# Last MLP of a two-layer trunk: blocks of the down projection in pairs, by seven products each

## The chip, the cores and the metric

One core of a Trainium2 chip runs the whole program. The metric is the time of one execution on the device in microseconds (us), the median of several runs.

## The reference, cut to what matters

Two layers; each has a token mixer and an MLP with squared ReLU. All data are float32; x is 512 tokens by 1024, the MLP's hidden width is 4096. The change is in the second layer's MLP, the last stage before the output:

```python
shift, scale, gate = ada_mod(c, ada_w[layer, 1], ada_b[layer, 1])    # three rows of 1024; gate has 1 added
u = x * (1.0 + scale) + shift
y = jnp.square(jax.nn.relu(u @ mlp_w1[layer] + mlp_b1[layer])) @ mlp_w2[layer] + mlp_b2[layer]
x = layer_norm(ALPHA * x + gate * y, ln_g[layer, 1], ln_b[layer, 1])
```

## The kernel before

Every large product is made of three: an operand x is split into a high part (a cast to float32r, on ACT) and a low part (x less its high part, on DVE), and PE adds up high x high, high x low and low x high in PSUM (`mm3`). A matmul multiplies a 128x128 block with 128x512.

`mlp` goes through the hidden width in eight blocks of 512. `up(b)` makes four chunks of 128 hidden units for all 512 tokens, 24 matmuls each; ACT makes relu (`r`) and its square, rounded, as high part (`hh`); DVE squares `r` again (`h`) and takes the low part (`hl`). `down(b)` multiplies them with 512 rows of w2: for each of four groups of 128 tokens and both halves of the 1024 columns twelve matmuls, 96 for the block, and DVE adds each result to `Y`. `up(b)` stands ahead of `down(b - 1)`.

Weights come in a list that `plan_weights` writes, a megabyte an entry. `w_dma` loads one into one of two buffers (`ws`), `w_pre` splits it (tiles `wh` and `wl`, four of 128x1024 each, or 128x512 tiles of the common pool `s2` for the entries in `wsmall`), `w_take` hands it to PE. The DMAs are all issued on SP's queue, in order; a load waits there for its buffer.

Beside the blocks run two things: `self.later` holds the residual (X times ALPHA times the norm's row, plus a row; 16 POOL steps on 128x512), taken up by `self.step`, two a chunk, so in block 1. `self.ada` holds the gate's sums over c (`ada_steps`, loads `ast`, sums `acc`, one half on DVE, one on ACT and POOL), taken up by `self.tick` from block 1 on; PE adds up over partitions at the end (`pada`). In the last block w2 is multiplied by the gate on POOL, and `Y` too, so that `down(7)` can add straight to X.

The pools give out buffers as they become free. The order within each engine is set by the scheduler of the tile layer, from the order in which the code issues and its own estimate of times; so instructions stand otherwise than in the code. All lines of the profile are L50, the helper's.

Of the kernel before, what the change touches and what calls it, by code (L numbers as in the profile page):

```python
# [8 lines left out]
F32 = mybir.dt.float32  # L9
F32R = mybir.dt.float32r  # L10
# [3 lines left out]
ALU = mybir.AluOpType  # L14
# [4 lines left out]
P = 128  # L19
D = 1024  # L20
S = 512
NT = S // P
# [12 lines left out]
WS_BUFS = 2  # L35
S2_BUFS = 42
PRED = mybir.dt.uint32


class InOrder:  # L40
# [33 lines left out]
class Trunk:  # L74
# [19 lines left out]
    def s2(self, name, dtype=F32):  # L94
        return self.sp.tile([P, S], dtype, tag="s2", name=name)
# [220 lines left out]
    def plan_weights(self):  # L316
        i = self.i
        L = []
        win = i["ev_w_in"][0]
        L += [("ch", win, 1024, 256), ("ch", win, 1280, 256), ("tok", win, 1536), ("tok", win, 1792),  # L320
              ("ch", win, 2048, 256), ("ch", win, 2304, 256), ("ch", win, 640, 128), ("ch", win, 768, 256)]

        def out(w, n):
            for h in range(2):
                for b in range(2):
                    L.append(("half", w, h, b, n))

        def mlp(l):
            w1, w2 = i["mlp_w1"][l], i["mlp_w2"][l]
            up = lambda b: [("ch", w1, b * 512, 256), ("ch", w1, b * 512 + 256, 256)]  # L330
            dn = lambda b: [("rows", w2, b * 512, 2 * l + 1), ("rows", w2, b * 512 + 256, 2 * l + 1)]
            L.extend(up(0))
            for b in range(1, 8):
                L.extend(up(b) + dn(b - 1))
            L.extend(dn(7))

        self.wsmall = set()

        def alternate(n0):
            for q in range(n0, len(L)):  # L340
                if (q - n0) // 2 % 2:
                    self.wsmall.add(q)

        n0 = len(L)
        out(i["ev_w_out"][0], 0)
        mlp(0)
        alternate(n0)
# [7 lines left out]
        out(i["od_w_out"][0], 2)  # L355
        mlp(1)
        alternate(n0)
        self.wlist, self.n_dma, self.n_split, self.n_take = L, 0, 0, 0
        self.wstage, self.wready = {}, {}

    def w_dma(self):
        d = self.wlist[self.n_dma]
        kind, w = d[0], d[1]
        if kind == "ch":
# [34 lines left out]
    def w_pre(self, eng=None):  # L399

        nc = self.nc
        if self.n_split >= len(self.wlist):
            return
        while self.n_dma < min(self.n_split + WS_BUFS, len(self.wlist)):
            self.w_dma()
        d = self.wlist[self.n_split]
        st = self.wstage.pop(self.n_split)
        kind = d[0]
        small = self.n_split in self.wsmall
# [18 lines left out]
        self.n_split += 1  # L428

    def w_take(self):  # L430
# [325 lines left out]
    def even(self):  # L756
# [341 lines left out]
    def mlp(self, l, X, rest, last):  # L1098
        nc, i = self.nc, self.i
        n = 2 * l + 1  # L1100
        nb = 8

        def up(b):
            hh, hl = self.u8("hh"), self.u8("hl")
            ws = self.w_take() + self.w_take()
# [10 lines left out]
            for f in range(4):  # L1116
                if b == 0:
                    part(f, 2, 4)
                else:
                    self.proj_ch(pts[f], ws[f])  # L1120
                if f % 2 == 0:
                    self.w_pre()
                col = 64 + l * 32 + b * 4 + f
                r, h2 = self.s2("r"), self.s2("h2")
                nc.scalar.activation(r, pts[f], AF.Relu, bias=self.colA[:, col:col + 1])
                nc.scalar.activation(hh[:, f], r, AF.Square)
                nc.vector.tensor_tensor(h2, r, r, op=ALU.mult)
                nc.vector.tensor_tensor(hl[:, f], h2, hh[:, f].bitcast(F32), op=ALU.subtract)
                if b:
                    self.step(2)  # L1130
                    if f % 2:
                        self.tick()
            return hh, hl

        def down(b, hh, hl, mid=None, after=None, byhalf=False):
            ws = self.w_take() + self.w_take()
            for t in range(NT):
# [26 lines left out]
                if not byhalf:  # L1164
                    for h in range(2):
                        nc.vector.tensor_tensor(Y[t][h], Y[t][h] if b else b2[h], pts[h], op=ALU.add)
                        if b == nb - 2:
                            nc.gpsimd.tensor_tensor(Y[t][h], Y[t][h], self.gates[n][h], op=ALU.mult)
                            nc.gpsimd.tensor_tensor(X[t][h], X[t][h], Y[t][h], op=ALU.add)
                else:  # L1170
# [5 lines left out]
                    self.tick()  # L1176

        b2 = self.bc(i["mlp_b2"][l:l + 1, :], f"b2{l}")
        Y = [[self.s2(f"Y{t}_{h}") for h in range(2)] for t in range(NT)]
        prev = up(0)  # L1180
        for b in range(1, nb):
            if b == 1 and last:
                self.ada = [self.ada_steps([(3, 4)], "g", True), self.ada_steps([(3, 5)], "v", True)]
            cur = up(b)
            down(b - 1, *prev)
            prev = cur
        self.tick(99)
        if last:
            g = self.bc(i["ln_g"][1, 1:2, :], "fg")
# [407 lines left out]
```

## Time and profile before

| | us |
|---|---|
| three runs | 1262.27, 1263.17, 1264.21 |
| profiled execution | 1266.51 |
| its span, first to last instruction | 1264.8 |
| PE / DVE / ACT / POOL busy in it | 1224.6 / 908.8 / 590.2 / 512.9 |
| granted TensorE clock, mean | 0.994 of 2.4 GHz |

The last MLP begins at about 901 us. A matmul's listed time overlaps the next one's: the distance of two starts says what one costs. The same holds for DVE and ACT, with a smaller overlap.

### The profile page before, as it was taken

The numbers are of one execution on the slowest core, as the hardware profiler recorded it, in microseconds if no ns is written. First come the engines' busy times: TensorE is split into PE (matmuls) and PEld (weight loads), VectorE is DVE, ScalarE is ACT, GpSimd is POOL, SyncE is SP. The second block draws the span as 40 slices with busy tenths as digits, with TensorE's granted clock in tenths as the row PEclk, the third lists the DMA queues.
The fourth block names the chain that finished last, engine by engine and source line by source line (L and its number), as shares of the span: only waits on it lengthen the run. The fifth ranks groups of instructions, "written<-read, shape, count | busy, mean of one in ns | idle before, by whom it ended". The sixth has DMA issues, their size and how long they took to land. (4 is left out here: it accounts for less than half of the span.)

```text
span 1264.8 us, 17847 instructions
## 1 busy us (share of the span) xinstructions
PE 1224.6 (97%) x6543; PEld 1044.2 (83%) x6543; DVE 908.8 (72%) x1423; ACT 590.2 (47%) x1044; POOL 512.9 (41%) x524
## 2 busy tenths in 40 slices
PE   6999899999999999999999999999899999999997
PEld 5787678888888888888999999887888788888886
DVE  7689898768877866879578878778768744543656
ACT  3476653452453544432567767753453342322321
POOL 3665523346330321474266558558437000000166
PEclk9999999999999999999999999999999999999999
DMA  9657416163666466524232332343262624232311
GB/s 316 186 199 267 173 61 198 56 230 119 240 224 233 145 195 227 182 67 124 81 101 85 92 93 52 113 153 106 79 233 72 211 67 133 81 117 70 133 34 67
DMA packets 126409, 177.52 MB, mean 140 GB/s; under 512 B 9270, under 2 KB 82644, under 8 KB 126322
## 3 DMA queue, kind: packets, MB, share of 16 engines
q1 hardware_dynamic: 126210, 176.33, 42.4%
q8 instruction: 52, 0.85, 0.3%
q14 instruction: 35, 0.29, 0.1%
q10 hardware_dynamic: 112, 0.05, 0.0%
HBM read 172.10 MB, written 4.26 MB: 139 GB/s over the span
## 5 line engine op out<-in xcount | busy, mean ns | idle before, releaser
L50 DVE TENSOR_TENSOR wl<-ws,wh 128x512 fp32r<-128x512 f32 (+1 forms) x255 | 269.3, 1081 | 67.7 <-ACT wh L50 63.4
L50 ACT CAST wh<-ws 128x1024 fp32r<-128x1024 f32 (+2 forms) x271 | 207.5, 808 | 200.5 <-PE p L50 81.4
L50 PE MATMUL p<-uh,wh 128*128 128x512 f32 (+1 forms) x576 | 206.2, 366 | 0.0
L50 PE MATMUL p<-uh,wl 128*128 128x512 f32 (+1 forms) x576 | 205.9, 365 | 0.0
L50 PE MATMUL p<-wh,hh 128*128 128x512 f32 (+1 forms) x516 | 201.0, 390 | 0.0
L50 PE MATMUL p<-wh,hl 128*128 128x512 f32 (+1 forms) x516 | 200.0, 388 | 0.0
L50 PE MATMUL p<-wl,hh 128*128 128x512 f32 (+1 forms) x516 | 199.9, 387 | 0.0
L50 PE MATMUL p<-ul,wh 128*128 128x512 f32 (+1 forms) x576 | 192.9, 366 | 0.0
L50 POOL TENSOR_TENSOR acc<-acc,ast 128x512 f32<-128x512 f32 x70 | 102.9, 1470 | 203.3 <-ACT ast L50 108.4
L50 DVE TENSOR_TENSOR h<-r 128x512 f32<-128x512 f32 x64 | 53.6, 840 | 123.6 <-ACT r L50 123.6
L50 PEld LDWEIGHTS p<-uh,wl 128*128 128x128 f32 x576 | 108.6, 189 | 17.5
L50 PEld LDWEIGHTS p<-uh,wh 128*128 128x128 f32 x576 | 108.6, 189 | 17.6
L50 PEld LDWEIGHTS p<-ul,wh 128*128 128x128 f32 x576 | 100.9, 189 | 17.4
L50 PEld LDWEIGHTS p<-wh,hh 128*128 128x128 f32 x516 | 96.9, 188 | 20.3 <-issue 0.2
L50 PEld LDWEIGHTS p<-wl,hh 128*128 128x128 f32 x516 | 96.9, 188 | 20.2 <-issue 0.5
L50 PEld LDWEIGHTS p<-wh,hl 128*128 128x128 f32 x516 | 96.9, 188 | 19.8
L50 ACT ACTIVATE r<-p,colA 128x512 f32<-128x512 f32 x64 | 43.8, 684 | 148.7 <-PE p L50 148.7
L50 POOL TENSOR_TENSOR ws<-ws,gate 128x512 f32<-128x512 f32 x16 | 25.0, 1597 | 210.6 <-DMA ws<-in_mlp_w_dram 210.6
L50 DVE TENSOR_TENSOR Y<-Y,p 128x512 f32<-128x512 f32 x96 | 64.8, 681 | 41.0 <-PE p L50 40.3
L50 ACT ACTIVATE ast<-ast,cs 128x512 f32<-128x512 f32 x70 | 49.9, 721 | 91.3 <-DMA ast<-in_ada_w_dram 91.3
L50 DVE SCALAR_TENSOR_TENSOR acc<-ast,cs,acc 128x512 f32<-128x512 f32 x70 | 82.5, 1179 | 13.2 <-DMA ast<-in_ada_w_dram 12.7
L50 POOL TENSOR_TENSOR ul<-u,uh 128x512 fp32r<-128x512 f32 x32 | 45.0, 1418 | 74.0 <-ACT uh L50 65.4
(320 smaller groups left out, 2681.2 us busy)
## 6 DMA issues: line engine op xcount, KB each, us to landing
ws<-in_mlp_w_dram SPq DMA_DIRECT2D x64, 1024.0 KB
ast<-in_ada_w_dram SPq DMA_DIRECT2D x160, 256.0 KB
ws<-in_od_w_in_dram SPq DMA_DIRECT2D x16, 1024.0 KB
ast<-in_ada_w_dram SPq DMA_DIRECT2D x16, 512.0 KB
ws<-in_ev_w_in_dram SPq DMA_DIRECT2D x7, 1024.0 KB
ws<-in_ev_w_out_dram SPq DMA_DIRECT2D x4, 1024.0 KB
nf<-fd SPq DMA_DIRECT2D x16, 256.0 KB
ws<-in_od_w_out_dram SPq DMA_DIRECT2D x4, 1024.0 KB
```

The costliest lines, as they stand in the source:

```text
L50: x = f(*a, **k)
```

## The change

In the last MLP blocks 0 to 5 are taken in three pairs. A pair's down projection is 512 tokens x 1024 hidden x 1024 columns; cut in half each way it is eight products of 256 x 512 x 512, and `winograd` makes it with seven, in Winograd's form of Strassen's method. Each product has a factor of the hidden values (`A11, S3, S1, S2, A12, A22, S4`) and one of the weights (`B11, T3, T1, T2, B21, T4, B22`); S and T are sums and differences of the quarters. `up(b, raw)` leaves the squares unsplit in float32 (`hr`), since sums are formed first; `factor` forms and splits them (`ha`, or `hah` and `hal`). `wino_b` forms and splits the weights' factors, with a second copy of one quarter (`wE`), loaded once more. Four pairs of PSUM banks hold the products; three are added to a second time. DVE adds the results to `acc` (U2, Q7, Q5, C11, D21, D12), and eight additions after the third pair make `Y` of them. Blocks 6 and 7 stay as they were, but now `up(6)` and `up(7)` stand together.

The residual steps move to blocks 2 and 3 (counted from 0), one a chunk; the gate's sums are taken up in blocks 4 to 6. Up weights of all blocks but 1 and 7 are split in tiles of 128x1024. The first MLP stays.

```diff
+WINOGRAD = (1,)
+WINO_B = ("B11", "T3", "T1", "T2", "B21", "T4", "B22")
+WINO_A = ("A11", "S3", "S1", "S2", "A12", "A22", "S4")
+WINO_SRC = {"B11": (0, 0), "T3": (0, 1), "B21": (1, 0), "B22": (1, 1)}
...
+            if l in WINOGRAD:
+                for g in range(0, 6, 2):
+                    L.extend(up(g) + up(g + 1) + [("wino", w2, g * 512, x) for x in WINO_B])
+                L.extend(up(6) + up(7) + dn(6) + dn(7))
+                for b in (n0 + 2, len(L) - 6, len(L) - 2):
+                    self.wsmall |= {b, b + 1}
+                return
...
+    def wino_b(self, which, st):
...
+        if which == "B11":
+            self.wB11 = st
+        elif which == "T3":
+            self.wE, self.wB12 = self.wE_next, st
+            for k in range(4):
+                sub(self.wE[k], self.wE[k], st[:, k])
+        if which == "T1":
+            for a in (0, 2):
+                x = self.wB12[:, a:a + 2, :]
+                sub(x, x, self.wB11[:, a:a + 2, :])
+                r += halves(self.wB12, a)
+            for k in range(4):
+                nc.vector.tensor_tensor(self.wE[k], self.wE[k], self.wB11[:, k], op=ALU.add)
+            return r
+        for a in (0, 2):
+            r += halves(self.wE if which in ("T3", "T2", "T4") else st, a)
+        if which == "B21":
+            for k in range(4):
+                sub(self.wE[k], st[:, k], self.wE[k])
+        return r
...
+            for q, (bank, on, to, bias) in enumerate(plan):
+                if len(ops) < min(q + 3, 7):
+                    ops.append(factor(WINO_A[len(ops)], H, len(ops)))
+                w = self.w_take()
+                self.w_pre()
+                if not on:
+                    pts[bank] = [self.ps("p2") for _ in range(2)]
+                for k in range(4):
+                    for t in range(2):
+                        tok = slice(t * P, t * P + P)
+                        lh, ll = [x[:, tok] for x in ops[q][k]]
+                        for n3, (x, y) in enumerate(((lh, w[k][0]), (lh, w[k][1]), (ll, w[k][0]))):
+                            nc.tensor.matmul(pts[bank][t], x, y, start=(not on and k == 0 and n3 == 0),
+                                             stop=(k == 3 and n3 == 2), skip_group_check=True)
...
+            for g in range(0, 6, 2):
+                H = [up(g, True)[0], None]
+                first = [factor(WINO_A[q], H, q) for q in range(2)]
+                H[1] = up(g + 1, True)[0]
+                if g == 2:
+                    self.ada = [self.ada_steps([(3, 4)], "g", True), self.ada_steps([(3, 5)], "v", True)]
+                winograd(g, acc, H, first)
```

What stands in the engines' order at the places that matter, before and after (names are tiles, numbers tell them apart; `p2` is a PSUM bank of the down projection):

PE before, the start of a token group of `down` in block 1: `wh`, `wl` weights, `hh`, `hl` hidden values.

```order
L50 MATMUL p2_10406<-wh_10200,hh_9795 128x512
L50 MATMUL p2_10406<-wl_10201,hh_9795 128x512
L50 MATMUL p2_10406<-wh_10200,hl_9796 128x512
L50 MATMUL p2_10407<-wh_10200,hh_9795 128x512
L50 MATMUL p2_10407<-wl_10201,hh_9795 128x512
L50 MATMUL p2_10407<-wh_10200,hl_9796 128x512
```

PE now, the start of the second pair's third product (T1 in `wh_10568`, S1 in `hah` and `hal`; p2_10719 and p2_10720 are the fourth product's):

```order
L55 MATMUL p2_10669<-wh_10568,hah_10557 128x512
L55 MATMUL p2_10669<-wl_10569,hah_10557 128x512
L55 MATMUL p2_10670<-wh_10568,hah_10557 128x512
L55 MATMUL p2_10670<-wl_10569,hah_10557 128x512
L55 MATMUL p2_10719<-wh_10614,ha_10609 128x512
L55 MATMUL p2_10720<-wh_10614,ha_10609 128x512
L55 MATMUL p2_10669<-wh_10568,hal_10558 128x512
L55 MATMUL p2_10670<-wh_10568,hal_10558 128x512
```

Matmuls with S1's low part have moved behind those with its high part and behind two of the next product.

DVE before, the gate's sum `acc` and the gate itself in `up(2)` (`h`, `hl` hidden values):

```order
L50 TENSOR_TENSOR h_10209<-r 128x512
L50 SCALAR_TENSOR_TENSOR acc_5_9989<-ast_5_3_0_10162,cs,acc_5_9989 128x512
L50 TENSOR_TENSOR hl<-h_10209,hh 128x512
L50 SCALAR_TENSOR_TENSOR acc_5_9989<-ast_5_3_1_10164,cs,acc_5_9989 128x512
L50 TENSOR_TENSOR h_10239<-r 128x512
L50 TENSOR_TENSOR hl<-h_10239,hh 128x512
```

DVE now, the same last two steps of `acc`, at the start of the third pair's products (`hr<-hr` form S2 and S1, `wl<-ws` is T1, `U` an accumulator, `ha` S2's low part, `hal` S1's):

```order
L55 TENSOR_TENSOR hr<-hr 128x4x256
L55 SCALAR_TENSOR_TENSOR acc_5_11012<-ast_5_3_0_11191,cs,acc_5_11012 128x512
L55 TENSOR_TENSOR hr<-hr 128x4x256
L55 TENSOR_TENSOR wl<-ws,wh 128x1024
L55 TENSOR_TENSOR U_9978<-U_9978,p_11221 128x512
L55 SCALAR_TENSOR_TENSOR acc_5_11012<-ast_5_3_1_11193,cs,acc_5_11012 128x512
L55 TENSOR_TENSOR U_9980<-U_9980,p_11222 128x512
L55 TENSOR_TENSOR wl<-ws,wh 128x1024
L55 TENSOR_TENSOR ha<-hr,ha 128x1024
L55 TENSOR_TENSOR hal<-hr,hah 128x512 x2
```

They have moved from an up phase to the place between S1's steps and the split of its low part.

ACT before, one block's last chunks and the casts behind them:

```order
L50 ACTIVATE r<-p_10778,colA 128x512
L50 ACTIVATE hh<-r 128x512
L50 ACTIVATE r<-p_10779,colA 128x512
L50 ACTIVATE hh<-r 128x512
L50 CAST wh<-ws 128x512 x8
```

ACT now, the last two chunks ahead of the third pair's products (`wE_11031`, `wE_11032` are T3's second half, `ast` the gate's loads):

```order
L55 ACTIVATE r<-p_11025,colA 128x512
L55 ACTIVATE hr<-r 128x512
L55 CAST wh<-wE_11031 128x512
L55 CAST wh<-wE_11032 128x512
L55 ACTIVATE r<-p_11026,colA 128x512
L55 ACTIVATE hr<-r 128x512
L55 ACTIVATE ast_4_3_0_11183<-ast_4_3_0_11183,cs 128x512
L55 ACTIVATE ast_4_3_1_11185<-ast_4_3_1_11185,cs 128x512
L55 CAST wh<-ws 128x1024 x2
```

Casts of weights have moved ahead of the last chunk's relu, and two of the gate's products stand behind its square.

## Rows read from the trace of the kernel before

**Rows 1.** Page: busy us (share) and count; tenths in 40 slices.

```profile
PE 1224.6 (97%) x6543; PEld 1044.2 (83%) x6543; DVE 908.8 (72%) x1423; ACT 590.2 (47%) x1044; POOL 512.9 (41%) x524
...
PE   6999899999999999999999999999899999999997
...
DVE  7689898768877866879578878778768744543656
```

**Rows 2.** Chain that ended last: start us, us, engine, tile, count.

```profile
995.14 255.74 PE p L50 x1128
...
1250.97 0.70 DVE X L50
```

**Rows 3.** Timeline of PE and ACT: start us, us, engine, instruction, idle before.

```profile
1060.31 0.39 PE L50 MATMUL p<-uh,wh 128*128 128x512 f32 x1
...
1065.74 0.39 PE L50 MATMUL p<-uh,wh 128*128 128x512 f32 x1
...
1059.14 1.06 ACT L50 CAST wh<-ws 128x1024 fp32r<-128x1024 f32 x1 [0.30 <-PE p L50]
...
1065.94 0.69 ACT L50 ACTIVATE r<-p,colA 128x512 f32<-128x512 f32 x1 [4.38 <-PE p L50]
1066.67 0.64 ACT L50 ACTIVATE hh<-r 128x512 fp32r<-128x512 f32 x1
...
1083.53 4.25 ACT L50 CAST wh<-ws 128x512 fp32r<-128x512 f32 x8
```

**Rows 4.** Timeline of DVE in the same block.

```profile
1060.61 1.22 DVE L50 TENSOR_TENSOR wl<-ws,wh 128x1024 fp32r<-128x1024 f32 x1
1061.75 0.68 DVE L50 TENSOR_TENSOR Y<-Y,p 128x512 f32<-128x512 f32 x1
...
1066.67 0.69 DVE L50 TENSOR_TENSOR h<-r 128x512 f32<-128x512 f32 x1 [3.10 <-ACT r L50]
1067.46 0.69 DVE L50 TENSOR_TENSOR hl<-h,hh 128x512 fp32r<-128x512 f32 x1
...
1084.39 2.49 DVE L50 TENSOR_TENSOR wl<-ws,wh 128x512 fp32r<-128x512 f32 x4
```

**Rows 5.** Timeline of PE at the gate's sums.

```profile
992.20 1.12 PE L50 MATMUL pada<-acc,ones 128*128 128x512 f32 x2 [0.58 <-POOL acc L50]
...
994.01 1.12 PE L50 MATMUL pada<-acc,ones 128*128 128x512 f32 x2 [0.69 <-DVE acc L50]
```

**Rows 6.** Timeline of POOL and DVE, with POOL busy and, last row, idle.

```profile
952.37 13.37 POOL L50 TENSOR_TENSOR X<-X,rB 128x512 f32<-128x512 f32 x8
...
989.16 2.99 POOL L50 TENSOR_TENSOR acc<-acc,ast 128x512 f32<-128x512 f32 x2 [13.57 <-ACT ast L50]
...
959.41 1.77 DVE L50 TENSOR_TENSOR wl<-ws,wh 128x512 fp32r<-128x512 f32 x1
961.11 1.78 DVE L50 SCALAR_TENSOR_TENSOR acc<-ast,cs,acc 128x512 f32<-128x512 f32 x1
...
976.65 0.74 DVE L50 SCALAR_TENSOR_TENSOR acc<-ast,cs,acc 128x512 f32<-128x512 f32 x1
```

**Rows 7.** Timeline of SP's issues and ACT: a weight load and its first cast.

```profile
978.02 3.84 SPq L50 DMA_DIRECT2D ws<-in_mlp_w_dram  x2
...
982.95 2.00 ACT L50 CAST wh<-ws 128x1024 fp32r<-128x1024 f32 x2 [6.44 <-DMA ws<-in_mlp_w_dram]
```

**Rows 8.** Timeline of PE after its longest wait near the last MLP.

```profile
889.71 1.30 PE L50 MATMUL pt<-ident,X 128*128 128x128 f32 x8 [3.26 <-DVE X L50]
...
891.23 0.63 PE L50 MATMUL pw<-wl,mh 128*128 128x512 f32 x1
891.66 0.63 PE L50 MATMUL pw<-wh,ml 128*128 128x512 f32 x1
...
894.08 0.40 PE L50 MATMUL pw<-wh,ml 128*128 128x512 f32 x1
```

More of the change, by code (lines that the diff above doesn't have):

```diff
@@ L321, in plan_weights, with alternate @@
               ("ch", win, 2048, 256), ("ch", win, 2304, 256), ("ch", win, 640, 128), ("ch", win, 768, 256)]
+        self.wsmall = set()
+        def alternate(n0):
+            for q in range(n0, len(L)):
+                if (q - n0) // 2 % 2:
+                    self.wsmall.add(q)
         def out(w, n):
@@ L335, in mlp @@
             L.extend(dn(7))
[L337 to L342, printed above, removed]
+            alternate(n0)
         n0 = len(L)
         out(i["ev_w_out"][0], 0)
+        alternate(n0)
         mlp(0)
-        alternate(n0)
         win = i["od_w_in"][0]
@@ L355, in plan_weights @@
         out(i["od_w_out"][0], 2)
+        alternate(n0)
         mlp(1)
-        alternate(n0)
         self.wlist, self.n_dma, self.n_split, self.n_take = L, 0, 0, 0
@@ L363, in w_dma @@
         kind, w = d[0], d[1]
+        if kind == "wino":
+            return self.wino_dma(*d[1:])
         if kind == "ch":
@@ L408, in w_pre @@
         kind = d[0]
+        if kind == "wino":
+            self.wready[self.n_split] = self.wino_b(d[3], st)
+            self.n_split += 1
+            return
         small = self.n_split in self.wsmall
@@ L428, in w_pre, with wino_dma, halves @@
         self.n_split += 1
+    def wino_dma(self, w, r0, which):
+        nc = self.nc
+        block = lambda r, c: w[r:r + 512, c:c + 512].rearrange("(k p) f -> p k f", p=P)
+        st = None
+        if which in WINO_SRC:
+            r, c = WINO_SRC[which]
+            st = self.wp.tile([P, 4, 512], F32, tag="ws", bufs=WS_BUFS, name="ws")
+            nc.sync.dma_start(st, block(r0 + 512 * r, 512 * c))
+        if which == "T3":
+            E = [self.s2(f"wE{k}") for k in range(4)]
+            for k in range(4):
+                nc.sync.dma_start(E[k], w[r0 + 512 + k * P:r0 + 512 + k * P + P, 512:1024])
+            self.wE_next = E
+        self.wstage[self.n_dma] = st
+        self.n_dma += 1
+    def wino_b(self, which, st):
+        nc = self.nc
+        sub = lambda o, a, b: nc.vector.tensor_tensor(o, a, b, op=ALU.subtract)
+        r = []
+        def halves(src, a):
+            hi, lo = [self.wp.tile([P, 2, 512], F32R, tag=x, name=x) for x in ("wh", "wl")]
+            if isinstance(src, list):
+                for j in range(2):
+                    nc.scalar.copy(hi[:, j], src[a + j])
+                    sub(lo[:, j], src[a + j], hi[:, j].bitcast(F32))
+            else:
+                nc.scalar.copy(hi, src[:, a:a + 2, :])
+                sub(lo, src[:, a:a + 2, :], hi.bitcast(F32))
+            return [(hi[:, j], lo[:, j]) for j in range(2)]
+        if which == "B11":
[18 more added lines that the diff above has]
+        return r
     def w_take(self):
@@ L1116, in up @@
             for f in range(4):
+                if f == 2 and len(ws) < 4:
+                    ws = ws + self.w_take()
+                if f % 2 == 0 and b and raw:
+                    self.w_pre()
                 if b == 0:
@@ L1128, in up @@
-                nc.vector.tensor_tensor(hl[:, f], h2, hh[:, f].bitcast(F32), op=ALU.subtract)
-                if b:
+                if not raw:
+                    h2 = self.s2("h2")
+                    nc.vector.tensor_tensor(h2, r, r, op=ALU.mult)
+                    nc.vector.tensor_tensor(hl[:, f], h2, hh[:, f].bitcast(F32), op=ALU.subtract)
+                if raw:
+                    self.step(b > 1)
+                elif b:
                     self.step(2)
-                    if f % 2:
-                        self.tick()
+                if f % 2 and b and (l not in WINOGRAD or b > 3):
+                    self.tick()
@@ L1133, in up, with factor @@
             return hh, hl
+        def factor(name, H, q):
+            a = [H[0][:, :, 0:256], H[0][:, :, 256:512]] + ([H[1][:, :, 0:256], H[1][:, :, 256:512]] if H[1] else [])
+            sub = lambda o, x, y: nc.vector.tensor_tensor(o, x, y, op=ALU.subtract)
+            if q % 3 < 2:
+                t = self.u8("ha", F32R, (2, 4, 256))
+                parts = [(slice(0, 4), t[:, 0], t[:, 1])]
+            else:
+                parts = [(slice(f, f + 2), *[self.s2(x, F32R).rearrange("p (k t) -> p k t", k=2) for x in ("hah", "hal")])
+                         for f in (0, 2)]
+            if name == "S3":
+                sub(a[1], a[0], a[1])
+            elif name == "S1":
+                sub(a[1], a[3], a[1])
+                nc.vector.tensor_tensor(a[0], a[0], a[1], op=ALU.add)
+            elif name == "S4":
+                sub(a[2], a[2], a[1])
+            src = a[{"A11": 0, "S3": 1, "S1": 0, "S2": 1, "A12": 2, "A22": 3, "S4": 2}[name]]
+            terms = []
+            for fs, hi, lo in parts:
+                nc.scalar.copy(hi, src[:, fs])
+                sub(lo, src[:, fs], hi.bitcast(F32))
+                terms += [(hi[:, k], lo[:, k]) for k in range(fs.stop - fs.start)]
+            return terms
@@ new lines, in winograd @@
+        def winograd(g, acc, H, first):
+            ops = list(first)
+            pts = {}
+            plan = [("1", False, "U2", None), ("7", False, "Q7", None), ("5", False, "Q5", 1), ("6", False, "U2", None),
+                    ("1", True, "C11", 0), ("7", True, "D21", 0), ("5", True, "D12", 1)]
+            for q, (bank, on, to, bias) in enumerate(plan):
+                if len(ops) < min(q + 3, 7):
+                    ops.append(factor(WINO_A[len(ops)], H, len(ops)))
+                w = self.w_take()
+                self.w_pre()
+                if not on:
+                    pts[bank] = [self.ps("p2") for _ in range(2)]
+                for k in range(4):
+                    for t in range(2):
[4 more added lines that the diff above has]
+                                             stop=(k == 3 and n3 == 2), skip_group_check=True)
+                ops[q] = None
+                for t in range(2):
+                    if (to, t) in acc:
+                        nc.vector.tensor_tensor(acc[to, t], acc[to, t], pts[bank][t], op=ALU.add)
+                        continue
+                    acc[to, t] = self.s2(f"{to}{t}")
+                    if bias is None:
+                        nc.vector.tensor_copy(acc[to, t], pts[bank][t])
+                    else:
+                        nc.vector.tensor_tensor(acc[to, t], b2[bias], pts[bank][t], op=ALU.add)
@@ L1178, in mlp @@
         b2 = self.bc(i["mlp_b2"][l:l + 1, :], f"b2{l}")
[L1179 to L1185, printed above, removed]
-            prev = cur
+        if l in WINOGRAD:
+            acc = {}
+            for g in range(0, 6, 2):
[5 more added lines that the diff above has]
+                winograd(g, acc, H, first)
+            for t in range(2):
+                for x, y in (("D12", "U2"), ("D21", "U2"), ("Q7", "Q5"), ("Q7", "U2")):
+                    nc.vector.tensor_tensor(acc[x, t], acc[x, t], acc[y, t], op=ALU.add)
+            Y = [[acc["C11", t], acc["D12", t]] for t in range(2)] + [[acc["D21", t], acc["Q7", t]] for t in range(2)]
+            del acc
+            prev = up(6)
+            cur = up(7)
+            down(6, *prev)
+            prev = cur
+        else:
+            Y = [[self.s2(f"Y{t}_{h}") for h in range(2)] for t in range(NT)]
+            prev = up(0)
+            for b in range(1, nb):
+                cur = up(b)
+                down(b - 1, *prev)
+                prev = cur
         self.tick(99)
```

15 lines of the change are left out of this document (9 added, 6 removed).

## Prediction

> **What bounds the kernel now.** I read the page's share of busy time first: PE is busy 97% of the span and DVE 72%, and in the 40 slices PE stays at 9 through the last seven while DVE falls to 3 to 6 [rows 1]. A busy PE can hide waits, so I went to the chain that ended last. Its largest piece lies in the last MLP: 1128 matmuls in 255.74 us with nothing between them, then a few DVE steps to the end [rows 2]. That is 255.74 / 1128 = 0.2267 us a matmul of 512 columns; PE waits for nobody there, so each such matmul taken out should give back 0.2267 us, as long as PE goes on waiting for nobody. What could make it wait is DVE and ACT, which split weights and hidden values into high and low parts. Their costs I read from the timelines of one quiet block.
>
> ACT takes 0.53 us for a cast of 512 columns (eight in 4.25) and 1.06 for 1024; relu and square take 0.73 and 0.63, and relu starts 0.20 after the last matmul of its chunk (24 matmuls from 1060.31 to 1065.74, relu at 1065.94) [rows 3]. DVE lists 1.22 us for 1024 columns and 0.69 for 512, but its next instruction starts after 1.14 (1060.61 to 1061.75) and 0.60 (four in 2.49, less the overlap of the last); only a step that reads the one right in front of it starts after 0.79 (1066.67 to 1067.46) [rows 4].
>
> **What is removed.** A pair of blocks had 192 matmuls of down projection; seven products of 24 make 168. Three pairs: 72 matmuls, 72 x 0.2267 = **16.3 us** off PE, all of them on the chain [rows 2].
>
> Before, the gate's two column sums made PE wait 0.58 us for POOL and 0.69 for DVE at 992 and 994 [rows 5]. In the change the last of these sums stand on DVE and POOL in the third pair's first two products, and PE's two sums behind the last chunk of block 6, some 50 us later. The waits go: **1.3 us**. PE's own work for them stays.
>
> **What is added, and what covers it.** Per pair, DVE now has, by the order's rows, 27 instructions of 1024 columns and 42 of 512: 27 x 1.14 + 42 x 0.60 = 56.0 us; before it was 8 and 48, 37.9 us. PE needs 360 x 0.2267 = 81.6 us for the pair, so on average DVE still fits. But the work is uneven: in the seven products (7 x 5.44 = 38.1 us) DVE has 14 of 1024 and 32 of 512, 35.2 us. Cover is 2.9 us in all, so what decides is whether each operand is there in time. I added DVE's queue up in its printed order for the second pair, counting from the last up matmul (0). A weight tile can be refilled only when half of the product two before is done (four tiles of 1024), plus 0.2 us and the 1.0 us cast.
>
> - Two casts of T3 stand before the last relu on ACT, so the last hidden square is there at 2.4. DVE meanwhile splits T3's second half (to 2.3) and adds two rows of T2 (3.5), then S2's difference (4.6), T1's first half (5.8), S1's sum (6.9), U's sums (8.1), T1's second half (9.3), S2's low part (10.4), S1's two low parts (11.0, 11.6).
> - The third product starts at 10.9, but six matmuls that need no low part of S1 stand in front, so the first of the two is needed at 12.2: 1.2 us to spare.
> - Further on: T2 done at 16.4 (needed at 19.0), B21's first half 19.9 (22.2), its second 23.4 (needed with the fifth product's second half, 24.5), T4's 25.8 and 28.2 (27.7 and 29.9), B22's first half 29.3 (33.1), S4's low part 31.0 (34.0). The least slack is 1.0 us. **No stall** in the second pair.
>
> In the first pair, S1 stands ahead of T1 and T3 is ready early; the same sum leaves at least 2.3 us: **no stall**.
>
> The third pair is worse. Two of the gate's DVE steps (0.68 each) stand around S1's sum, eight sums that put the quadrants together follow (4.8 us), and POOL's last two ada additions run from 3.1 to 6.1, just where S1 is formed. While POOL adds, DVE's steps on two SBUF operands take 1.77 us where they take 0.69, and the gate step 1.78 where it takes 0.74 [rows 6]: 2.4 times as long. So S1's low part comes at 14.1 where it is needed at 12.2: 1.9 us; B21's second half and T4's second half lose 0.2 and 0.5 again. **Stall 2.6 us.** If the two POOL additions (2.99 us [rows 6]) fall elsewhere it is near 0.9.
>
> Costs that I set at nothing: a fifth megabyte of down weights a pair (wE). A megabyte lands 4.9 us after its issue (978.02 to the cast at 982.95) [rows 7]; the tightest buffer, B21's, can be issued when B11 is given back at 3.5 and is needed at 16.4. Cover 8 us; if it went, PE would wait for what is missing. On SP, B21's load stands behind eight ada loads in the third pair, which were issued an up phase earlier. The residual rows' POOL work (16 multiplies and adds, 13.37 us for eight [rows 6]) runs in the second pair's up matmuls, where DVE has 56.0 - 35.2 = 20.8 us of work for 8 x 5.44 = 43.5 us; in POOL's 27 us, slowed 2.4 times, it does 11 of them, and the other 10 have 16 us. The differences on 128x4x256 are in no row; I take 1.14, as for 1024 columns of two SBUF operands; the bounds are 1.06 (ACT's cast of as many columns [rows 3]) and 1.33 (1.14 with the 0.19 of a dependent step); with four a pair that is under 1 us either way. Products alternate two banks, as the down matmuls do over h; I see nothing dearer in them.
>
> **Sum**: -16.3 - 1.3 + 2.6 = -15.0 us. The profiled execution took 1266.51 us (span 1264.8), 0.26% over the median of three, 1263.17; no row of the last MLP depends on that difference, so I take the 15.0 off the median: 1263.2 - 15.0 = **1248.2 us**.
>
> **A rule of the skill against this.** The Trainium skill (VectorE: DVE Perf Modes, The DRAIN you can't avoid) says that the next DVE instruction doesn't start before the pipeline of the one in front has emptied, which would make each cost its whole listed time. This case's rows speak against it: starts lie 0.60 and 1.14 apart, with 0.69 and 1.22 listed [rows 4]. By that rule the sum would be the first rival's.
>
> **Rivals.**
> First: *DVE costs its listed time in a full queue*, 1.22 and 0.69. Seven products then hold 14 x 1.22 + 32 x 0.69 = 39.2 us for 38.1, DVE becomes the bound, and the same additions give 0.5, 1.6 and 6.3 us of stall: 8.4, net -9.2, 1254.0 us. For it: almost every step now waits for ACT or PE, and the rows with the short distances are few. Against it: at 1060.61 and 1061.75 the wait was there as well, and the distance stayed 1.14.
>
> Second, on the other side: *each step pays the dependent distance*, 0.79 and 1.33, since most now read what was just written by ACT, by PE or by DVE. The seven products hold 14 x 1.33 + 32 x 0.79 = 43.9 us; stalls come to 4.0, 5.5 and 10.9 us, 20.4 in all: net +2.8, 1266 us. With it goes the clock: after PE had been idle 3.26 us, its matmuls started 0.43 us apart (891.23 to 891.66), the 1.2 GHz level, and the seven starts up to 894.08 took 2.85 us for 7 x 0.2267 = 1.59 [rows 8]: 1.3 us on top of each such wait; with two or three of them 1269 to 1270. It decides from a mean of about 0.17 us a step above mine. Against it: the 0.79 stands only between h and hl.
>
> Third: *nothing to be measured*: loads of weights land late once a pair, for instance B21 after 18 us instead of 4.9, and 5 us of wait a pair eat the gain: 1263 us. The load's slack of 8 us speaks against it. That the change doesn't do what it says is out: PE's order is 72 rows of matmul shorter.
>
> **How the numbers follow.** Forecast 0.63 (1245.6 with no stall at all, up to 1251 with the stall doubled), first rival 0.23 (1251 to 1257), second 0.08, third 0.06. Within 0.2% (2.5 us, about what a measurement of this kernel can tell from no change) lies the third, less a little: 0.05; slower by more than that, the second and a rest of the third: 0.09; faster: 0.86. The range leaves out the two last rivals and the worst of the first: 1245.5 to 1256.0.
>
> **What would show it.** Right: in the last MLP matmuls 0.2267 us apart with gaps of under 1 us in the first two pairs, one of some 2 us ahead of the low part of S1 in the third; DVE without idle time in the products, its starts 1.14 and 0.60 apart; no wait at pada. Wrong: gaps ended by DVE (wl, hal, ha) in every pair, a granted clock under 1.0 in the products, DVE steps at more than their distance above, or gaps that a DMA of ws or wE ends.

## The result, and the profile after

The changed kernel took 1252.72 us, the kernel before beside it 1264.26 us (medians of six runs each): ratio 0.9911, 95% interval 0.9893 to 0.9930, so 11.3 us less (8.8 to 13.5). The sum had said 15.0 less, 1248.2 us; the measured time is 4.5 us above that and inside the range of 1245.5 to 1256.0, but in the part of it that was the first rival's (1251 to 1257).

The profile shown is of an execution of 1259.8 us (span 1258.1), the longest of the six. Its last MLP starts later than that of the kernel before, by an amount that differs between executions of one kernel: the first 512-column matmul of `up(1)` starts at 926.15 in the profile of before, at 929.14 here, at 927.19 in a second profile of the changed kernel (e0), and between 922.4 and 929.1 in all profiles below. I therefore compare **the stretch**: from that matmul to the end of the span. Before it is 1264.8 - 926.15 = 338.65 us, now 1258.1 - 929.14 = 328.96.

The page of the changed kernel, busy time and tenths in 40 slices, answers to [rows 1]:

```profile
PE 1212.8 (96%) x6471; PEld 1033.0 (82%) x6471; DVE 971.4 (77%) x1474; ACT 630.0 (50%) x1087; POOL 520.3 (41%) x524
...
PE   6899899999999999999999999999899999989997
...
DVE  6689988768878667778568778768968589499756
...
POOL 2665422438312321366257565558510270130256
```

PE has 72 matmuls fewer, DVE 51 instructions more; one slice of PE in the last seven fell to 8. The waits of PE from `up(1)` on (us in total, times, longest), and the rows where they end:

```profile
PE p L55 <- DVE hal L55: 4.9, 2, 3.3
```

```profile
1044.34 0.73 PE L55 MATMUL p<-wh,ha 128*128 128x512 f32 x2
1046.72 0.74 PE L55 MATMUL p<-wh,hal 128*128 128x512 f32 x2 [1.64 <-DVE hal L55]
1047.29 0.40 PE L55 MATMUL p<-wh,hah 128*128 128x512 f32 x1
1047.53 0.39 PE L55 MATMUL p<-wl,hah 128*128 128x512 f32 x1
...
1128.02 0.64 PE L55 MATMUL p<-wh,ha 128*128 128x512 f32 x2
1131.94 1.22 PE L55 MATMUL p<-wh,hal 128*128 128x512 f32 x2 [3.28 <-DVE hal L55]
1132.96 0.63 PE L55 MATMUL p<-wh,hah 128*128 128x512 f32 x1
1133.39 0.63 PE L55 MATMUL p<-wl,hah 128*128 128x512 f32 x1
...
1138.58 0.39 PE L55 MATMUL p<-wh,hal 128*128 128x512 f32 x1
1138.81 0.39 PE L55 MATMUL p<-wh,hah 128*128 128x512 f32 x1
```

Both waits stand at the low part of S1, where the sum had 1.2 us to spare in the second pair (its least was 1.0) and its main stall in the third. In the second pair two matmuls start at 1044.34, so the next was due at 1044.79 and started at 1046.72: 1.9 us lost, and behind it matmuls are 0.23 apart. In the third the next was due at 1128.47 and started at 1131.94: 3.5 lost. Behind that they are 0.43 apart to about 1138, the 1.2 GHz level (the granted clock from 1132 to 1138 is 0.50 of 2.4 GHz); the 20 matmuls from 1131.94 to 1139.49 took 7.55 us in place of 20 x 0.2267 = 4.53: another 3.0. In all 8.4 us, where the sum had 2.6. There is no wait in the first pair and none at `pada`, where [rows 5] had two; the chain that ended last passes it without a gap and answers to [rows 2]:

```profile
1131.94 50.78 PE p L55 x210
1182.72 1.72 PE pada L55 x4
1184.44 59.86 PE p L55 x264
```

Why `hal` is late is on DVE, POOL and SP. The second pair's up phase ends with the matmul at 1032.30:

```profile
946.47 46.46 SPq L55 DMA_DIRECT2D ws<-in_mlp_w_dram  x6
992.99 1.05 SPq L55 DMA_DIRECT2D rA<-in_ln_g_dram  x2
```

```profile
999.46 0.62 POOL L55 TENSOR_SCALAR rA<-rA 128x512 f32<-128x512 f32 x1 [79.35 <-DMA rA<-in_ln_g_dram]
...
1015.25 15.77 POOL L55 TENSOR_TENSOR X<-X,rB 128x512 f32<-128x512 f32 x8
```

```profile
1011.83 2.30 DVE L55 TENSOR_TENSOR wl<-ws,wh 128x1024 fp32r<-128x1024 f32 x1 [3.84 <-ACT wh L55]
...
1016.29 4.54 DVE L55 TENSOR_TENSOR ha<-hr,ha 128x1024 fp32r<-128x1024 f32 x2
...
1022.99 6.88 DVE L55 TENSOR_TENSOR wE<-wE,ws 128x512 f32<-128x512 f32 x4
...
1039.11 1.21 DVE L55 TENSOR_TENSOR hr<-hr 128x1024 f32<-128x1024 f32 x1
1040.25 1.21 DVE L55 TENSOR_TENSOR wl<-ws,wh 128x1024 fp32r<-128x1024 f32 x1
...
1045.98 1.28 DVE L55 TENSOR_TENSOR hal<-hr,hah 128x512 fp32r<-128x512 f32 x2
```

The residual's rows (`rA`) are issued at 993, behind six weight loads that wait 46 us on SP's queue for their buffers. POOL's work runs from 999.46 to 1031, and ends 1.3 us ahead of the products. Beside it DVE's starts are 2.23 us apart for 1024 columns and 1.70 for 512. DVE stands idle for 14.9 us between 991.3 and 1011.8, waiting for ACT's casts, and from there to `hal` at 1045.98 not at all. S2's difference (`hr` at 1039.11) starts 6.8 us after the last up matmul; the sum had it 3.5 after.

In the third pair the last up matmul is at 1115.99; POOL's gate additions lie around it:

```profile
1108.37 7.14 POOL L55 TENSOR_TENSOR acc<-acc,ast 128x512 f32<-128x512 f32 x2 [6.14 <-ACT ast L55]
1119.34 3.19 POOL L55 TENSOR_TENSOR acc<-acc,ast 128x512 f32<-128x512 f32 x2 [3.83 <-ACT ast L55]
```

```profile
1109.18 1.21 DVE L55 TENSOR_TENSOR ws<-ws 128x1024 f32<-128x1024 f32 x1
...
1111.46 1.21 DVE L55 TENSOR_TENSOR ws<-ws 128x1024 f32<-128x1024 f32 x1
1112.59 3.48 DVE L55 SCALAR_TENSOR_TENSOR acc<-ast,cs,acc 128x512 f32<-128x512 f32 x2
...
1119.60 3.48 DVE L55 TENSOR_TENSOR wE<-wE,ws 128x512 f32<-128x512 f32 x2
1123.01 1.21 DVE L55 TENSOR_TENSOR hr<-hr 128x1024 f32<-128x1024 f32 x1
```

Two pairs of DVE steps beside them (1112.59 and 1119.60) take 3.48 us where a quiet pair takes 1.2 to 1.4. S2's difference starts 7.0 us after the last up matmul.

### The profile page after: what moved, and what is told of

Its sections match the earlier page's. It is cut to its first block, busy times and chain, and to the rows that moved or that the text cites. A ratio compares the mean times of both kernels' runs of the same rounds, so it can differ in the third digit from the quotient of the medians.

```text
span 1258.1 us, 17788 instructions
## 1 busy us (share of the span) xinstructions
PE 1212.8 (96%) x6471; PEld 1033.0 (82%) x6471; DVE 971.4 (77%) x1474; ACT 630.0 (50%) x1087; POOL 520.3 (41%) x524
## 5 line engine op out<-in xcount | busy, mean ns | idle before, releaser
L55 DVE TENSOR_TENSOR wl<-ws,wh 128x1024 fp32r<-128x1024 f32 (+1 forms) x235 | 266.3, 1154 | 87.9 <-ACT wh L55 83.7
L55 PE MATMUL p<-wh,hh 128*128 128x512 f32 (+1 forms) x324 | 125.9, 389 | 0.0
L55 PE MATMUL p<-wh,hl 128*128 128x512 f32 (+1 forms) x324 | 125.3, 387 | 0.0
L55 PE MATMUL p<-wl,hh 128*128 128x512 f32 (+1 forms) x324 | 125.2, 387 | 0.0
L55 DVE SCALAR_TENSOR_TENSOR acc<-ast,cs,acc 128x512 f32<-128x512 f32 x70 | 82.0, 1171 | 11.3 <-DMA ast<-in_ada_w_dram 10.8
L55 PE MATMUL p<-wh,ha 128*128 128x512 f32 x240 | 75.2, 390 | 0.0
L55 DVE TENSOR_TENSOR h<-r 128x512 f32<-128x512 f32 x40 | 34.5, 865 | 52.1 <-ACT r L55 52.0
L55 PE MATMUL pqk<-wh,uh 128*128 128x256 f32 x256 | 74.1, 290 | 0.0
L55 PE MATMUL pqk<-wh,ul 128*128 128x256 f32 x256 | 72.5, 284 | 0.0
L55 PE MATMUL pqk<-wl,uh 128*128 128x256 f32 x256 | 72.4, 283 | 0.0
L55 PEld LDWEIGHTS p<-wl,hh 128*128 128x128 f32 x324 | 60.9, 188 | 12.5 <-issue 0.2
```

Source lines behind the costliest of these rows:

```text
L55: x = f(*a, **k)
```

## The experiments

Theory A: DVE comes late into the products because POOL's work on two SBUF operands, moved next to them, slows it. Theory B: DVE's queue in the products is too full in itself. Gains are against the kernel before on the same chip; the interval is of the ratio.

| kernel | median us | ratio, 95% | stretch us | PE's waits from `up(1)` on, us |
|---|---|---|---|---|
| before | 1264.26 | | 338.65 | 0.6, 0.7 (`pada`) |
| changed | 1252.72 | 0.9911 (0.9893-0.9930) | 328.96 | 1.6, 3.3 (`hal`) |
| e0, again | 1254.25 | 0.9920 (0.9901-0.9939) | 327.41 | the same |
| e1, residual in block 6 | 1255.19 | 0.9927 (0.9910-0.9945) | 329.35 | 3.3 (`hal`) |
| e2, gate on DVE | 1248.67 | 0.9883 (0.9862-0.9903) | 323.49 | 1.6 (`hal`), 0.9 (`wl`) |
| e3, both | 1249.51 | 0.9889 (0.9868-0.9909) | 325.61 | 0.9 (`wl`) |
| e4, two pairs | 1254.71 | 0.9929 (0.9911-0.9948) | 328.26 | 1.6 (`hal`) |
| e6, moves alone | 1262.88 | 0.9994 (0.9983-1.0005) | 336.79 | none |
| e7, e2 and residual on DVE | 1249.26 | 0.9886 (0.9867-0.9904) | 321.54 | 0.9 (`wl`) |
| e8, e3 with residual on DVE | 1247.16 | 0.9871 (0.9850-0.9892) | 321.55 | 0.9 (`wl`) |
| e10, e2 and residual rows early | 1256.67 | 0.9943 (0.9923-0.9964) | 329.58 | 5.4 (`wl`, 7), 1.2 (`hal`) |
| e11, e7 and S1 longer | 1253.44 | 0.9921 (0.9901-0.9941) | 326.04 | 2.7 (`hah`), 0.9 (`wl`) |
| e12, e8 and gate spread | 1246.61 | 0.9871 (0.9850-0.9892) | 320.36 | none |

The medians carry what lies ahead of the stretch, which differs by some us from run to run; where the table's two columns differ by 1 or 2 us, the stretch and its waits decide. Each stretch is of one profiled execution: e7 and e8 agree within 0.01 us, the changed kernel's two profiles differ by 1.5. In all rows but two (changed, e3) the median gains less on the kernel before than the stretch does, by 0.5 to 3.6 us; where that lies is not shown.

**e0, the changed kernel again.**

> The changed kernel once more, on the same chip as the next three, so that they have something to be compared with. Its first profile had two waits of PE for DVE's `hal` (the low part of S1): 1.64 us in the second pair (about 2.0 us lost) and 3.28 us in the third, followed by matmuls 0.43 us apart for some 4 us (about 6.4 us lost). Both theories expect the same here: some 11 us under the kernel before, and the two waits again, within some tenths. If the waits differ by more than 1 us from profile to profile, they are no fixed place in the order, and both theories fall.

The waits came back at the same places, 4.8 us in all for 4.9. The stretch is 1.5 us shorter than in the first profile, 1.2 of it behind the third pair's wait: the clock stayed at the lower level for fewer matmuls.

**e1, the residual's steps in block 6.**

```diff
-                if raw:
-                    self.step(b > 1)
-                elif b:
+                if b and not raw:
                     self.step(2)
```

> The residual's 16 steps go from blocks 2 and 3 to block 6, two a chunk; all else stays. Theory A (carry-over): POOL's two-operand steps in the second pair's up phase slow DVE, which enters the products about 3 us late, and so `hal` is late. Then the second pair's wait goes (a loss of 2.0 us becomes under 0.3), DVE's steps in that up phase take 0.69 and 1.22 us instead of 1.7 and 2.3, and the kernel is 2 us faster than the changed one, if block 6, which has less for DVE to do, covers POOL's work. Theory B (the product's queue is too full in itself): the wait in the second pair stays at 1.5 us or more, and the time is that of the changed kernel within 0.5 us. The third pair keeps its loss of about 6 us by both.

The second pair's wait is gone, as A has it; DVE's S2 and S1 stand at their quiet places:

```profile
1028.88 1.22 DVE L55 TENSOR_TENSOR hr<-hr 128x1024 f32<-128x1024 f32 x1
...
1035.75 1.29 DVE L55 TENSOR_TENSOR hal<-hr,hah 128x512 fp32r<-128x512 f32 x2
```

But the kernel isn't faster; that part of my expectation fell. From `up(1)` to the last matmul it is 1.8 us shorter than e0 (317.14 for 318.97), and the tail behind the last matmul 3.8 longer (12.21 for 8.44). POOL's work of block 6 pushed the gate's products and the sums for X back, and in the tail one step of DVE met four steps of POOL in a row:

```profile
1236.03 2.55 POOL L55 TENSOR_TENSOR X<-X,fg 128x512 f32<-128x512 f32 x2
...
1238.52 2.52 POOL L55 TENSOR_TENSOR X<-X,fb 128x512 f32<-128x512 f32 x2
```

```profile
1236.08 5.52 DVE L55 SCALAR_TENSOR_TENSOR X<-X,mv,fg 128x512 f32<-128x512 f32 x1
```

The step ended 0.5 us after POOL did; in e0 it took 1.82. The gain was given back at the end, by the same contention.

**e2, the whole gate on DVE.**

```diff
-                    self.ada = [self.ada_steps([(3, 4)], "g", True), self.ada_steps([(3, 5)], "v", True)]
+                    self.ada = [self.ada_steps([(3, 4)], "v", True), self.ada_steps([(3, 5)], "v", True)]
```

> The half of the gate's sums that ACT and POOL made goes to DVE as the other half: no additions on POOL, 8 more steps of 0.74 us on DVE (5.9 us), spread from block 4 to block 6. Theory A: what makes `hal` late in the third pair is that POOL's additions slow DVE at the start of its products, not the number of DVE's steps; so the wait falls from 3.3 to 1 or 2 us in spite of more steps, the clock doesn't fall behind it, and the pair's loss goes from 6.4 to 1 to 2.5 us: 4 us faster than the changed kernel. Theory B (the queue is too full): 2 to 4 more steps of 0.74 around S1 make the wait longer by 1.5 to 3 us: 1.5 to 3 us slower than the changed kernel. The second pair keeps its 2.0 us by both.

DVE has eight steps more, and PE waits less: the third pair's 3.3 us for `hal` became 0.9 for T2's low part (the matmul that waits reads S2's `ha`, and the step of DVE that ends in front of it is the first of two `wl<-wE`), and behind it the matmuls stayed 0.23 us apart. The stretch is 3.9 us shorter than e0's. A expected 4; B expected it longer. The edit also takes eight steps off ACT, but that is not what helped: in the changed kernel DVE had under 0.1 us of idle time from 1105.6 to `hal` at 1131.21, so it was not waiting for ACT there. PE's waits in the stretch, and the second of them:

```profile
PE p L55 <- DVE hal L55: 1.6, 1, 1.6
PE p L55 <- DVE wl L55: 0.9, 1, 0.9
```

```profile
1122.82 0.50 PE L55 MATMUL p<-wl,ha 128*128 128x512 f32 x1 [0.91 <-DVE wl L55]
...
1122.08 1.29 DVE L55 TENSOR_TENSOR wl<-wE,wh 128x512 fp32r<-128x512 f32 x2
```

**e3, both edits.**

> Both of the edits before it: the residual in block 6 and the whole gate on DVE, so that POOL does nothing beside DVE in the second pair's up phase and at the start of the third pair's products. Theory A: the two gains add up, 5 to 6 us under the changed kernel, 16 to 17 us under the kernel before, which is what the 72 matmuls alone give; the clock stays at 2.4 GHz through all three pairs. Theory B: not faster than the changed kernel by more than 1 us, with waits for `hal` in both pairs.

The waits add up as A has them: only the 0.9 is left. The tail took back 4 us as in e1 (12.54 us), so the time is e2's, and the gain on the changed kernel is 4.7 us beside e0 where A had 5 to 6.

**e4, only two pairs.** The list of weights and the loop over blocks 4 to 7 change with the line shown.

```diff
-                for g in range(0, 6, 2):
+                for g in range(0, 4, 2):
```

> Only blocks 0 to 3 are taken in pairs; blocks 4 to 7 stay as in the kernel before; residual and gate as in the changed kernel. What it tells is what a pair is worth where DVE keeps up. Theory A: two pairs take 48 x 0.2267 = 10.9 us off PE, the waits at pada go (1.3), the second pair still loses 2.0 us, and the third pair's loss of some 6.4 us isn't there: 10.9 + 1.3 - 2.0 = 10.2 under the kernel before, so within 1.5 us of the changed kernel, which has a pair more. If instead a pair of products were worth less than its matmuls (dearer matmuls at two banks, say), it would be nearer to the kernel before than 8 us. The waits for `hal`: one, of 1.6 us.

With a pair less the time is the changed kernel's. By the parts 338.65 - 10.9 - 1.9 (e6) + 2.0 = 327.9; measured 328.26. A pair of products is worth its matmuls; the third one just paid for its own waits.

**e6, the moves alone**, in the kernel before: residual steps in blocks 2 and 3, gate from block 4 on.

> The kernel before with the two moves alone: residual steps one a chunk in blocks 2 and 3, the gate's sums taken up from block 4 on; no products are saved. The sum on record gave 1.3 us for the waits at pada that go. Theory A: in blocks of the old kind DVE has room for POOL's disturbance, so the moves cost nothing there, and the kernel is 1 to 2 us faster than before, or within what can be told. If the residual's move alone cost 2 us and the gate's more (theory C: the moves cost time wherever they stand, products or not), it would be 2 us or more slower.

No waits, and the stretch is 1.9 us shorter. The median (0.9994) can't tell that from nothing, and doesn't contradict it. Theory C is out: among blocks of the old kind the same moves cost nothing.

**e7, the residual on DVE**, in its old place, with e2's gate.

```diff
-            nc.gpsimd.tensor_tensor(X[t][h], X[t][h], rows[0][h], op=ALU.mult)
-            nc.gpsimd.tensor_tensor(X[t][h], X[t][h], rows[1][h], op=ALU.add)
+            e = nc.vector if n == 3 else nc.gpsimd
+            e.tensor_tensor(X[t][h], X[t][h], rows[0][h], op=ALU.mult)
+            e.tensor_tensor(X[t][h], X[t][h], rows[1][h], op=ALU.add)
```

> The gate on DVE as in e2, and the residual's 16 steps of blocks 2 and 3 on DVE in place of POOL; the scheduler puts them in one run in the second half of the second pair's up phase. DVE gets 16 x 0.60 = 9.6 us more there (20.8 + 9.6 = 30.4 of 43.5 us), and nobody slows it. Theory A: it is POOL's work beside DVE, not the work as such: the second pair's wait of 1.6 us goes although DVE does more, POOL's tail stays short, and the kernel is 2 us faster than e2, 1246.5 to 1247.5 us, 16 to 17 us under before. Rival: DVE still comes late into the products because the run of 16 stands in front of T3's and T2's steps; then the wait for `hal` stays at 1 us or more and the time is that of e2.

The second pair's wait went although DVE did 16 steps more in that phase, and did them in 11.1 us (6.15 + 1.88 + 3.08) where POOL took 27 (four scalings of the rows stay on POOL in both):

```profile
994.50 6.15 DVE L55 TENSOR_TENSOR X<-X,rA 128x512 f32<-128x512 f32 x8 [3.45 <-POOL rA L55]
1000.58 1.88 DVE L55 TENSOR_TENSOR X<-X,rB 128x512 f32<-128x512 f32 x3
...
1003.52 3.08 DVE L55 TENSOR_TENSOR X<-X,rB 128x512 f32<-128x512 f32 x5
```

The stretch is 1.95 us shorter than e2's, and the profiled execution's span is 1245.0 us, e12's 1244.9. The median doesn't show it (1249.26 beside e2's 1248.67, on another chip), so the 2 us that A expected in time did not come; what hides them I haven't found. This is the plainest evidence against B: more work on DVE, nearly none of POOL's beside it, no wait for `hal`.

**e8, the residual in block 6 on DVE**, with e3's other edits.

> As e3 (residual in block 6, gate on DVE), but with the residual's 16 steps on DVE, none on POOL. In e1 and e3 the second pair's wait was gone and no time was won: a DVE step on two SBUF operands in the last rows took 5.5 us where the changed kernel has 1.8, beside POOL additions that ran 13 us later than there. Theory: POOL, 13 us late after its 16 steps in block 6, is the cause; with these on DVE POOL is back at its old times, that step takes 1.8 us again, the last rows are 4 us shorter, and the kernel is 3 to 5 us faster than e3's 1249.5: about 1246. Rival: something else in the last block makes that step long; then the time stays at e3's.

The tail is 8.46 us again, the stretch 4.1 us shorter than e3's and equal to e7's; the median is 2.4 us under e3's, where 3 to 5 were expected. POOL's lateness was the cause of the long tail.

**e10, the residual's rows loaded early.** POOL keeps the residual; the rows are loaded in block 1, the steps issued in block 2.

```diff
+        if n == 3:
+            self.later.append(lambda: rows.extend(self.residual_rows(n)))
...
-                    self.step(b > 1)
+                    self.step(2 * (b == 2) + (b == 1 and f == 1))
```

> The gate on DVE as in e2; the residual stays on POOL in the second pair's up phase, but its two rows are loaded in block 1 (they stood on SP's queue behind six weight loads and came 6 us late), and its steps are issued two a chunk in block 2. So POOL does the same work beside DVE, only some 10 us earlier. Theory A in its narrow form (not how much POOL does, but how late): POOL is done about 15 us before the products, DVE has free time behind it to catch up, and the second pair's wait of 1.6 us goes; from up(1)'s first matmul to the end of the span 321.5 to 322 us, as with the residual on DVE. Rival: any 27 us of POOL's work in that up phase makes DVE late, wherever it lies; then the wait stays above 1 us and the stretch at 323.5.

It came out otherwise. With the rows there, the scheduler put POOL's steps not into block 2 but at once, into the first pair, across the start of its products:

```profile
951.70 16.38 POOL L55 TENSOR_TENSOR X<-X,rB 128x512 f32<-128x512 f32 x8
```

```profile
PE p L55 <- DVE wl L55: 5.4, 7, 1.4
PE p L55 <- DVE hal L55: 1.2, 1, 1.2
```

The second pair's wait is gone, and the first pair, which never waited, now waits seven times (six times for `wl` and once for `hal`; the seventh for `wl` is the third pair's 0.9). The wait follows POOL's work. Whether POOL's work at the very front of the second pair's up phase would be free was not settled by this run.

**e11, S1's formation longer.**

```diff
                 sub(a[1], a[3], a[1])
+                for _ in range(2 if self.pair == 2 else 0):
+                    nc.vector.tensor_tensor(a[1], a[1], a[1], op=ALU.max)
                 nc.vector.tensor_tensor(a[0], a[0], a[1], op=ALU.add)
```

> As e7 (residual and gate on DVE, no wait for `hal` in the second pair), with two more DVE steps of 128x4x256 in the second pair alone, between S2's difference and S1's sum (the maximum of S2 with itself, which changes no value): 2 x 1.14 = 2.3 us, 2.7 if each pays the 0.19 of a dependent step. It measures the slack that the sum on record gave for S1's low part, 1.2 us. If the slack is that, PE waits 1.1 to 1.5 us for `hal` and the stretch from up(1)'s first matmul to the end is 1.1 to 1.7 us longer than in e7 (321.54). If it waits the whole 2.3, there was no slack and the sum was right by chance; if it doesn't wait, there was twice as much.

It doesn't measure the slack: the scheduler also put T1's second half and others ahead of S1's sum, which so came at 1042.37, and PE waited for S1's high part instead.

```profile
1044.38 0.80 PE L55 MATMUL p<-wh,hah 128*128 128x512 f32 x1 [2.69 <-ACT hah L55]
1044.97 0.63 PE L55 MATMUL p<-wl,hah 128*128 128x512 f32 x1
1045.40 0.63 PE L55 MATMUL p<-wh,hah 128*128 128x512 f32 x1
```

The slack can be read in e7:

```profile
1029.89 1.22 DVE L55 TENSOR_TENSOR hr<-hr 128x1024 f32<-128x1024 f32 x1
...
1036.76 1.28 DVE L55 TENSOR_TENSOR hal<-hr,hah 128x512 fp32r<-128x512 f32 x2
```

```profile
1039.09 0.62 PE L55 MATMUL p<-wh,hal 128*128 128x512 f32 x2
```

`hal`'s first half starts at 1036.76 and is done some 0.6 later, and its first matmul starts unhindered at 1039.09. That is 1.7 us, for 1.2 in the sum. What the run does show is a price: 2.3 us more DVE work, in the order that the scheduler made of it, made the stretch 4.5 longer, by the wait and by eight matmuls 0.43 apart behind it.

**e12, the gate's sums spread**, one piece a block from block 2 on.

```diff
-                if f % 2 and b and (l not in WINOGRAD or b > 3):
+                if f % 2 and b and l not in WINOGRAD or f == 1 and b > 1 and l in WINOGRAD:
...
-                if g == 2:
+                if g == 0:
                     self.ada = [self.ada_steps([(3, 4)], "v", True), self.ada_steps([(3, 5)], "v", True)]
```

> As e8 (residual on DVE in block 6, gate on DVE), with the gate's sums taken up from block 2 on, one piece a block, so that all 16 DVE steps lie in the up phases of the second and third pair and none in their products. By the account so far the third pair's last wait (0.9 us for `wl` at T1) comes from four of these steps at the start of its products. Then it goes, PE waits for nothing from up(1) to the last rows, and that stretch takes 320.5 us, which is the kernel before's 338.65 less 16.3 for 72 matmuls and less the 1.9 that the moves alone gave; the kernel is at 1246 us or less, the fastest. If the steps only move the wait to the second pair, the stretch stays at 321.5 or more.

The stretch is 320.36 us, PE waits for nothing, and the chain that ended last goes through all three pairs in one piece:

```profile
910.32 270.10 PE p L55 x1248
1180.42 1.72 PE pada L55 x4
1182.14 48.98 PE p L55 x216
```

With 1246.61 us (ratio 0.9871, 0.9850 to 0.9892) it is faster than both kernels: 16 us under the kernel before (the 1246 that I expected at most is missed by 0.6). The wait that went was for T2's low part, not T1's.

## Why the prediction was right or wrong

**The matmuls, -16.3: right.** e12 has all that the change adds and no waits: 338.65 - 320.36 = 18.3, less e6's 1.9 for the moves, is 16.4.

**The waits at `pada`, -1.3: right in kind, 0.6 too small.** e6 gives 1.9 in the stretch. I took only the two listed waits of [rows 5]. The rest lies at the same place: from the last matmul of the up phase to the second one behind the `pada` sums PE took 3.98 us in the kernel before (991.23 to 995.21) and 2.18 in e6 (1118.75 to 1120.93), 1.8 less. A listed wait counts only from the listed end of the matmul in front, which lies 0.16 behind the time at which the next could have started.

**The first pair, no stall: right.** It doesn't wait, as long as POOL stays away (e10).

**The second pair, no stall: wrong, 2.0 us.** The sum of DVE's queue itself held. Where DVE is quiet, S2's difference starts 3.3 us and S1's low part 10.1 us after the last up matmul (e7: 1029.89 and 1036.76 after 1026.62), for 3.5 and an end at 11.0 in the sum. The step that failed is the residual under "costs that I set at nothing": "in POOL's 27 us, slowed 2.4 times, it does 11 of them, and the other 10 have 16 us". I averaged over the phase, having said of the products that an average tells little. POOL took 31.6 us, not 27 (26.9 for the 16 steps, the rest for four scalings of the rows and the pauses between, which I hadn't counted), and began 10 us late, since its rows stood on SP's queue behind six weight loads; so its work covered the half of the phase where DVE's queue is dense. DVE's 14.9 us of idle time lay in front, before 1011.8, and no 16 us were left behind POOL. I had looked at SP's queue for B21's load and not for the rows. That POOL's work made the wait is shown (e1, e7); that an earlier start alone would have spared it is not (e10).

**The third pair, 2.6: too small by 3 to 4 us.** POOL's last two additions came at 3.3 to 6.5 us after the last up matmul, as the sum had it (3.1 to 6.1). But the sum let them meet S1, with DVE on time until then. DVE was 1.5 us late already, from the two additions before, at 1108 to 1115, beside the gate's steps (it began to split T3's second half 2.4 us after the last up matmul, in e2 0.9); so these two met T2's sums, and S1 came behind them. That is 3.5 us in place of 1.9. The rest is the clock: it fell behind this wait and cost 1.8 us (e0) to 3.0. I had priced that in a rival only ([rows 8], 1.3 us) and not in the forecast's own stall. The sum's other line, 0.9 us if POOL's additions fall elsewhere, has the size of e2's wait by chance: that one is at T2's `wl` and with more DVE steps. Together, in the stretch: -16.3 - 1.9 + 8.4 = -9.8, and measured 328.96 - 338.65 = -9.7.

**The first rival** had the size (8.4 us of stall, 1254.0 us) and not the cause; that the time lies in the range is owed to the range's taking in most of this rival's band. In the full queue DVE's starts stay 1.14 apart with 1.21 listed (1039.11 to 1040.25 above). By the Trainium skill's rule (VectorE: DVE Perf Modes, The DRAIN you can't avoid) that the next step doesn't start until the pipeline is empty each would have cost its whole time; the trace after speaks against that as [rows 4] did. The same section adds that a next step which is not held (its word for one that must wait for all earlier ones) starts earlier, and with that the trace agrees. **The second rival** is out by the same rows, **the third** too: no gap ends with a load of weights.

**The cost of 128x4x256** that no row had: 1.14, as taken.

## What to carry to other kernels

When DVE becomes nearly full in a stage, look first at what POOL does beside it, and at the phase just ahead: here POOL's steps on two SBUF operands cost each such step of DVE beside a long run of them 1.1 us, and DVE did the same 16 steps in less than half of POOL's time. Say for each moved step when it can begin (its loads' place in the queue), not only in which phase it is issued; the mean cover of a phase says little where the consumer's work is dense at its end. And price the clock into every wait of several us on PE, in the forecast too.

## What the runs showed of the hardware

POOL beside DVE isn't a factor, as I had it (2.4), but an addition for each step: beside a long run of POOL's TENSOR_TENSOR, DVE's steps on two SBUF operands took 1.1 us more whatever their length, 2.23 from start to start for 1.14 at 1024 columns (4.54 listed for two) and 1.70 for 0.60 at 512 (6.88 for four). POOL's own starts in that run are also 2.23 and then 1.70 apart (15.77 for eight), where three steps with an idle DVE beside them are 1.25 apart: each engine did one step while the other did one. But it was not always one for one. In e1's tail a single step of DVE took 5.52 us, through four steps of POOL; and in the changed kernel's third pair POOL's addition at 1108.37 took 5.45 us while four steps of DVE, from 1108.58 to 1112.59, passed at their quiet distances.

The Trainium skill (SBUF — State Buffer, Who interferes with whom) says that a DVE instruction with two SBUF inputs contends with a GpSimd (POOL) instruction that reads SBUF, and that the port pair they share is an exclusive lock. The run of one step each agrees with a lock; that one side loses four turns in a row doesn't follow from it. What decides who gets the next turn stays open.

Behind waits of PE of 2.69 us (e11) and 3.3 (changed kernel, e0, e1) its matmuls ran 0.43 us apart for a few us, at a granted clock of 0.50 (1044.4 to 1047.5 in e11, 1131 to 1134 in e0); behind those of 1.64 and 0.91 not. The same wait at the same place cost 1.8 us of clock in one profile and 3.0 in the other.
